# Attention scores of the later blocks as two 64-row products instead of one padded product; first projections 512 columns wide

## The chip, the cores and the metric

The kernel runs on one core of a Trainium2 chip. The metric is the device time of one execution in microseconds (us), the median of several runs. Every time below comes from these runs or from one profiled execution of the kernel before.

## The reference

The model takes 512 tokens of width 1024 through three layers. The first has four mixers (two kinds of attention, two recurrences), a gated merge of them and a mixture of 32 experts. The other two are "hybrid layers", and the change lies in them:

```python
h = rms_norm(x, norm_mix_g)
proj = h @ w_in
rq, rk, rv, rg, pv, nq, nk, nv, mq = jnp.split(proj, 9, axis=-1)       # 256 columns each
# retention on rq, rk, rv, rg; pooling on pv
na = neighbourhood_attention(rms_norm(nq), rms_norm(nk), nv, na_rpb)    # 4 heads of 64
mo = memory_attention(rms_norm(mq), rms_norm(mk), mv)                   # 4 heads of 64, 256 memory rows
up = jnp.einsum('bsnc,ncd->bsnd', branches, w_branch)
gates = jax.nn.sigmoid(h @ w_gate).reshape(b, s, N_BRANCH, dm)
x = x + jnp.einsum('bsnd,bsnd->bsd', gates, up) @ w_out
a, g = jnp.split(rms_norm(x, norm_ffn_g) @ w_ffn_in, 2, axis=-1)
x = x + (jax.nn.silu(a) * g) @ w_ffn_out
```

Both attentions are a softmax of q k / 8 (plus a bias in the neighbourhood) times v. In the neighbourhood attention the 512 tokens are a grid of 8 rows by 64 columns: a block of 8 x 16 queries (128 tokens) sees a window of 8 x 32 keys (256 tokens), so there are 4 blocks.

## The kernel before

Activations lie with features on the partitions, 128 at a time, and tokens along the free axis. A head has 64 features, so one 128-partition tile holds two heads (z = 0 in partitions 0 to 63, z = 1 in 64 to 127).

**Projections.** Weights come by DMA in pieces of 1 MB (`load_w`) and are split into a high and a low part (`split`, L278 on ScalarE, L280 on VectorE). Each product is then three: `mm3` issues L286, L287 and L288. The first projection of a hybrid layer starts while the norm of the layer before it is still running, token tile by token tile: `first_tok(c)` (L1761) takes 512 columns of `w_in` (the keys and values of the retention), as two loads of all 1024 rows by 256 columns, and for each of 4 token tiles adds up two halves of 256 columns in one PSUM bank named `tm`. It is called once per hybrid layer. The bank is 512 columns wide.

**Attention scores.** Two scores, for z = 0 and z = 1, are one product: the query tile is the stationary operand with its 128 partitions (both heads), and the keys stand in a padded tile, `nkz` or `mkz`, that holds keys of z = 0 in partitions 0 to 63 with zeros below, and beside it keys of z = 1 in partitions 64 to 127 with zeros above. The product is 128 rows by 512 columns in one PSUM bank: 256 columns for each head. `nkz` is zeroed by GpSimd (L2142) and filled by ScalarE (L2150, through `proj_tok` and `head_norm`); `mkz` is zeroed (L2236) and filled (L2238) by GpSimd. The neighbourhood score is L2175 (product `ns`), the memory score L2243 (`ms`, its maximum on VectorE at L2246). There are 8 of each in a layer: 4 token blocks times 2 pairs of heads. An fp32 product appears in the trace as two records.

After its score each pair of heads goes through `probs` (L2194): scale, four transposes (`pT`, L2207), and the value products (`po`, L2219), in steps that other work may come between.

**Scores of the first layer.** There the scores of two heads are two products of 64 contracted rows each (L1134, product `s`), into two banks.

**Order.** The merge's products, `gate` (h times w_gate) and `up` (branches times w_branch), are produced by a generator that runs through the whole attention part of a layer; they are 128x512 and three per product. Which instruction stands where on an engine is settled when the program is built: a scheduler orders the instructions by an estimate of their times, by the dependencies and by the order of the code, and the memory attention is issued with raised priority (L1886). Each engine then runs its own list in order and waits at an instruction for what it needs. PSUM has 8 banks, in three groups of buffers: "mm" 2, "ms" 4, "mg" 2 (L2262). Scores, `tm` of the first two token tiles and projections take "mm"; transposes and value products take "ms"; gate and up products take "mg".

Of the kernel before, what the change touches and what calls it, by code (L numbers as in the profile page):

```python
# [210 lines left out]
def backward(a):  # L211

    ap = [list(x) for x in a.ap]
    step, n = ap[-1]
    return bass.AP(tensor=a.tensor, offset=a.offset + step * (n - 1), ap=ap[:-1] + [[-step, n]])


class Kern:
# [1542 lines left out]
    def first_tok(self, c):  # L1761

        Ws = []
        for z in range(2):
            raw = self.load_w([(self.win[:, c + z * 256:c + z * 256 + 256], 0, 256)], KD, 256, z)
            Ws.append([self.split(raw[:, k:k + 4], z) for k in (0, 4)])
        out = []

        def f(i):
            p = self.ps("tm", tag=("mm", "mg")[i // 2])  # L1770
            s = slice(i * 128, (i + 1) * 128)
            for z, W in enumerate(Ws):
                for k in range(KD):
                    self.mm3(p[:, z * 256:(z + 1) * 256], (self.xH[:, k, s], self.xL[:, k, s]), (W[k // 4][0][:, k % 4], W[k // 4][1][:, k % 4]), k == 0, k == KD - 1)
            out.append(p)
        self.first(f)
        return out
# [342 lines left out]
    def neighbourhood(self, l, ctx):  # L2120
        tc, nc = self.tc, self.nc
        pp = ctx.enter_context(tc.tile_pool(name="np2", bufs=1, reuse_waits="tile"))
        f2 = ctx.enter_context(tc.tile_pool(name="nf2", bufs=3, reuse_waits="tile"))
        rp = self.A["rpb2"]
        namask = self.cst4(pp, "namask")[0]

        def biases(z):

            t = pp.tile([128, 8, 4, 32], F32, name="nab", tag="nab", bufs=2)
            for r in range(8):  # L2130
                nc.sync.dma_start(t[r * 16:(r + 1) * 16].rearrange("p a h b -> p (a h) b"),
                                  bass.AP(tensor=rp.tensor, offset=rp.offset + ((l * 15 + 7 - r) * 4) * 96 + 17 + 8 * z, ap=[[1, 16], [96, 32], [1, 32]]))
            for h in range(4):
                nc.vector.scalar_tensor_tensor(t[:, :, h], in0=t[:, :, h], scalar=-1.0,
                                               in1=namask[:, z * 256:(z + 1) * 256].rearrange("p (a b) -> p a b", a=8), op0=OP.mult, op1=OP.add)
            return t
        KS = (0, 8, 24, 32)

        qT = pp.tile([128, 2, 4, 8, 16], F32, name="nqT")

        kz = pp.tile([128, 2, 2, S], F32, name="nkz")
        nc.gpsimd.memset(kz, 0.0)  # L2142
        vT = pp.tile([128, 2, S], F32, name="nvT")
        gq, gk = self.row(pp, f"na_q_norm_g{l}"), self.row(pp, f"na_k_norm_g{l}")
        nc.vector.tensor_single_scalar(gq, gq, -0.125, OP.mult)
        self.proj_tok((1280, lambda i, p: self.head_norm(f2, p, gq, lambda t: [
            nc.scalar.activation(qT[:, j, :, 2 * i:2 * i + 2], t[:, j * 128:(j + 1) * 128].rearrange("p (r b c) -> p b r c", r=2, b=4), AF.Copy)
            for j in range(2)], None)))
        self.proj_tok((1536, lambda i, p: self.head_norm(f2, p, gk, lambda t: [
            nc.scalar.activation(kz[64 * z:64 * z + 64, :, z, i * 128:(i + 1) * 128], t[64 * z:64 * z + 64, 0:256].rearrange("p (a b) -> p a b", a=2), AF.Copy)  # L2150
            for z in range(2)], None)))
        for j, f in enumerate(self.fm(1792, "nv")):
            nc.scalar.activation(vT[:, j], f(), AF.Copy)
        self.flush()
        g8 = lambda t: t.rearrange("p (r c) -> p r c", r=8)
        bias, zb = None, None
        for cb in range(4):
            z = (0, 1, 1, 2)[cb]
            if z != zb:
                bias, zb = biases(z), z  # L2160

            vq = f2.tile([128, 2, 8, 32], F32, name="vq", bufs=2)
            for j in range(2):
                nc.gpsimd.tensor_copy(vq[:, j], g8(vT[:, j])[:, :, KS[cb]:KS[cb] + 32])
            vw = f2.tile([128, 2, 256], F32, name="vw", bufs=2)
            p = self.ps("vw")
            for hf in range(2):
                for j in range(2):
                    o = (hf * 2 + j) * 128
                    nc.tensor.transpose(p[:, o:o + 128], vq[:, j, 4 * hf:4 * hf + 4].rearrange("p r c -> p (r c)"), self.ident)  # L2170
            nc.scalar.activation(vw.rearrange("p a n -> p (a n)"), p, AF.Copy)
            def score(cb, j, bias):
                def f():
                    p = self.ps("ns", tag="mm")
                    nc.tensor.matmul(p, lhsT=qT[:, j, cb].rearrange("p r c -> p (r c)"), rhs=kz[:, j].rearrange("p z (r c) -> p z r c", r=8)[:, :, :, KS[cb]:KS[cb] + 32],  # L2175
                                     start=True, stop=True)
                    t = f2.tile([128, 2, 256], F32, name="nt", bufs=2)
                    mn, rs = (f2.tile([128, 2], F32, name=n) for n in ("nmn", "nrs"))
                    for z in range(2):
                        nc.vector.tensor_tensor_reduce(out=g8(t[:, z]), in0=g8(p[:, z * 256:(z + 1) * 256]), in1=backward(bias[:, :, 2 * j + z]), scale=1.0, scalar=3e38,  # L2180
                                                       op0=OP.add, op1=OP.min, accum_out=mn[:, z:z + 1])
                        nc.scalar.activation(t[:, z], t[:, z], AF.Exp, bias=mn[:, z:z + 1], scale=-1.0, accum_out=rs[:, z:z + 1])
                    return t, rs
                return f

            def done(p, cb=cb):
                H, L = (t.rearrange("p j (r c) -> p j r c", r=8)[:, :, :, cb * 16:cb * 16 + 16] for t in self.ys[2])
                self.done[2] = self.split_act(H, L, p.rearrange("p (j r c) -> p j r c", j=2, r=8))
            sh = []
            for j in range(2):  # L2190
                self.spawn(self.probs(j, f2, sh, score(cb, j, bias), lambda h, k, vw=vw: vw[:, k, h * 64:(h + 1) * 64], done))
        self.flush()
# [31 lines left out]
    def mem_attention(self, l, ctx):  # L2224
        tc, nc = self.tc, self.nc
        kT, v = self.kv[l]
        pp = ctx.enter_context(tc.tile_pool(name="mp2", bufs=1, reuse_waits="tile"))
        f2 = ctx.enter_context(tc.tile_pool(name="mf2", bufs=3, reuse_waits="tile"))
        qT = pp.tile([128, 2, S], F32, name="mqT")
        gq = self.row(pp, f"mem_q_norm_g{l}")  # L2230
        nc.vector.tensor_single_scalar(gq, gq, 0.125, OP.mult)
        self.proj_tok((2048, lambda i, p: self.head_norm(f2, p, gq, qT, slice(i * 128, (i + 1) * 128))))
        self.flush()

        kz = pp.tile([128, 2, 2, 256], F32, name="mkz")
        nc.gpsimd.memset(kz, 0.0)  # L2236
        for z in range(2):
            nc.gpsimd.tensor_copy(kz[64 * z:64 * z + 64, :, z], kT[64 * z:64 * z + 64])  # L2238

        def score(i, j):  # L2240
            def f():
                p = self.ps("ms", tag="mm")
                nc.tensor.matmul(p, lhsT=qT[:, j, i * 128:(i + 1) * 128], rhs=kz[:, j].rearrange("p z n -> p (z n)"), start=True, stop=True)  # L2243
                p = p.rearrange("p (z n) -> p z n", z=2)
                mn, rs = (f2.tile([128, 2], F32, name=n) for n in ("mmn", "mrs"))
                nc.vector.tensor_reduce(mn, p, axis=AX.X, op=OP.max, negate=True)  # L2246
                t = f2.tile([128, 2, 256], F32, name="mt")
                for z in range(2):
                    nc.scalar.activation(t[:, z], p[:, z], AF.Exp, bias=mn[:, z:z + 1], accum_out=rs[:, z:z + 1])
                return t, rs  # L2250
            return f
        for i in range(NT):
            sh = []
            cols = (slice(None), slice(i * 128, (i + 1) * 128))
            for j in range(2):
                self.spawn(self.probs(j, f2, sh, score(i, j), lambda h, k: v[:, k, h * 64:(h + 1) * 64],
                                      lambda p, cols=cols: self.put(3, cols, p.rearrange("p (a b) -> p a b", a=2))))
        self.flush()
# [24 lines left out]
```

## Time and profile before

| | |
|---|---|
| median of 3 runs | 2551.24 us (2550.71 to 2551.85) |
| profiled execution | 2550.32 us |
| span from its first to its last instruction | 2548.6 us |
| TensorE (PE) busy | 2479.9 us, 97% |
| VectorE (DVE) busy | 1086.0 us, 43% |
| ScalarE (ACT) busy | 794.8 us, 31% |
| GpSimd (POOL) busy | 347.9 us, 14% |
| granted TensorE clock, mean | 0.990 of 2.4 GHz |

A time in the trace counts from the first instruction. The recorded duration of a matmul includes its latency, and neighbours overlap: what a product takes of TensorE is read from the distance between the starts of the records around it. "x2" in a row stands for two records run together. The attention of the first hybrid layer lies around 1080 to 1180 us, that of the second around 1890 to 1990 us.

### The profile page before, as it was taken

The numbers are of one execution on the slowest core, as the hardware profiler recorded it, in microseconds if no ns is written. First come the engines' busy times: TensorE is split into PE (matmuls) and PEld (weight loads), VectorE is DVE, ScalarE is ACT, GpSimd is POOL, SyncE is SP. The second block draws the span as 40 slices with busy tenths as digits, with TensorE's granted clock in tenths as the row PEclk, the third lists the DMA queues.
The fourth block names the chain that finished last, engine by engine and source line by source line (L and its number), as shares of the span: only waits on it lengthen the run. The fifth ranks groups of instructions, "written<-read, shape, count | busy, mean of one in ns | idle before, by whom it ended". The sixth has DMA issues, their size and how long they took to land.

```text
span 2548.6 us, 32848 instructions
## 1 busy us (share of the span) xinstructions
PE 2479.9 (97%) x13340; PEld 1954.9 (77%) x13340; DVE 1086.0 (43%) x2002; ACT 794.8 (31%) x1362; POOL 347.9 (14%) x386
## 2 busy tenths in 40 slices
PE   9999999997988989999999999999999999999999
PEld 7788777686545569877788888889877777888887
DVE  3455569645212264344354333226444435433322
ACT  5331234432202233343233322214244223322311
POOL 1201210301102125311200000003421110000000
PEclk9999999998999999999999999999999999999999
DMA  5400321357999932523232322332241332322232
GB/s 159 148 18 18 108 76 50 133 188 279 401 416 353 375 108 79 107 43 107 83 116 83 99 84 93 105 108 75 88 88 51 108 100 99 100 83 93 89 99 83
DMA packets 220124, 324.41 MB, mean 127 GB/s; under 512 B 43384, under 2 KB 176408, under 8 KB 208192
## 3 DMA queue, kind: packets, MB, share of 16 engines
q1 hardware_dynamic: 214784, 311.76, 36.2%
q0 software_dynamic: 5184, 10.50, 1.1%
q8 instruction: 107, 1.75, 0.3%
q14 instruction: 49, 0.40, 0.0%
HBM read 313.81 MB, written 16.80 MB: 130 GB/s over the span
## 4 chain that ended last, share of the span: by engine, by line
PE 61%; DVE 1%; issue 1%; SPq 0%; POOL 0%; ACT 0%; DMA 0%; DVEq 0%; POOLq 0%
PE gate L288 5%; PE gate L286 4%; PE gate L287 4%; PE acc L287 4%; PE acc L286 4%; PE acc L288 4%; PE ffg L287 3%; PE ffg L286 3%; PE ffa L287 3%; PE ffa L286 3%; PE ffg L288 3%; PE ffa L288 3%; PE tm L286 2%; PE tm L288 2%; PE tm L287 2%; PE up L286 1%
## 5 line engine op out<-in xcount | busy, mean ns | idle before, releaser
L280 DVE TENSOR_TENSOR wl<-wraw,wh 128x1024 fp32r<-128x1024 f32 (+1 forms) x336 | 424.6, 1269 | 569.4 <-ACT wh L278 562.2
L278 ACT ACTIVATE wh<-wraw 128x1024 fp32r<-128x1024 f32 (+1 forms) x336 | 354.2, 1059 | 898.3 <-PE gate L287 188.7
L288 PE MATMUL gate<-hH,wl 128*128 128x512 f32 x512 | 204.9, 403 | 5.8 <-DVE wl L280 5.8
L286 PE MATMUL gate<-hH,wh 128*128 128x512 f32 x512 | 207.0, 404 | 0.0
L287 PE MATMUL gate<-hL,wh 128*128 128x512 f32 x512 | 206.7, 404 | 0.0
L1589 PE MATMUL hid<-mraw,xgt 128*64 128x256 f32 x1024 | 126.5, 393 | 16.4 <-DMA mraw<-moe_w_gate 9.0
L286 PE MATMUL acc<-wh,fH 128*128 128x512 f32 x352 | 136.8, 390 | 0.0
L287 PE MATMUL acc<-wl,fH 128*128 128x512 f32 x352 | 136.7, 389 | 0.0
L288 PE MATMUL acc<-wh,fL 128*128 128x512 f32 x352 | 136.6, 389 | 0.0
L286 PE MATMUL tm<-wh,hH 128*128 128x256 f32 x448 | 128.9, 288 | 4.7 <-DVE hn L1807 4.1
L288 PE MATMUL tm<-wh,hL 128*128 128x256 f32 x448 | 127.6, 286 | 0.2 <-DVE hL L296 0.2
L287 PE MATMUL tm<-wl,hH 128*128 128x256 f32 x448 | 126.8, 284 | 0.0
L287 PE MATMUL ffa<-hL,wh 128*128 128x512 f32 x320 | 126.6, 396 | 0.0
L288 PE MATMUL ffa<-hH,wl 128*128 128x512 f32 x320 | 126.6, 396 | 0.0
L286 PE MATMUL ffg<-hH,wh 128*128 128x512 f32 x320 | 126.6, 396 | 0.0
L287 PE MATMUL ffg<-hL,wh 128*128 128x512 f32 x320 | 126.6, 396 | 0.0
L288 PE MATMUL ffg<-hH,wl 128*128 128x512 f32 x320 | 126.6, 396 | 0.0
L286 PE MATMUL ffa<-hH,wh 128*128 128x512 f32 x320 | 126.5, 395 | 0.0
L1589 PEld LDWEIGHTS hid<-mraw,xgt 128*64 128x64 f32 x1024 | 76.1, 141 | 60.9 <-DMA mraw<-moe_w_gate 11.9
L288 PEld LDWEIGHTS gate<-hH,wl 128*128 128x128 f32 x512 | 96.2, 188 | 32.0 <-DVE wl L280 7.5
L286 PEld LDWEIGHTS gate<-hH,wh 128*128 128x128 f32 x512 | 96.2, 188 | 25.7 <-issue 4.2
L287 PEld LDWEIGHTS gate<-hL,wh 128*128 128x128 f32 x512 | 96.2, 188 | 24.7 <-issue 3.8
(600 smaller groups left out, 5109.7 us busy)
## 6 DMA issues: line engine op xcount, KB each, us to landing
wraw<-w_in SPq DMA_DIRECT2D x45, 1024.0 KB, 5.1
wraw<-w_ffn_in SPq DMA_DIRECT2D x44, 1024.0 KB, 5.0
wraw<-w_gate SPq DMA_DIRECT2D x32, 1024.0 KB, 8.1
mraw<-moe_w_gate SPq DMA_DIRECT2D x31, 1024.0 KB, 12.1
mraw<-moe_w_down SPq DMA_DIRECT2D x31, 1024.0 KB, 10.4
mraw<-moe_w_up SPq DMA_DIRECT2D x30, 1024.0 KB, 12.7
wraw<-w_ffn_out SPq DMA_DIRECT2D x20, 1024.0 KB, 5.0
wraw<-w_branch SPq DMA_DIRECT2D x12, 1024.0 KB, 5.5
```

Of the source, the lines that this page charges most:

```text
L278: self.last_split = nc.scalar.activation(H, raw, AF.Copy)
L280: self.after(nc.vector.tensor_sub(L, raw, H.bitcast(F32)), *hold)
L286: m = t.matmul(out, lhsT=lhs[0], rhs=rhs[0], start=first, stop=False)
L287: t.matmul(out, lhsT=lhs[0], rhs=rhs[1], start=False, stop=False)
L288: t.matmul(out, lhsT=lhs[1], rhs=rhs[0], start=False, stop=last)
L1589: m = nc.tensor.matmul(p[r, c], lhsT=lhs[:, k, r], rhs=w(k), start=k == 0, stop=k == KT - 1, skip_group_check=True)
```

## The change

- `first_tok` loads two pieces of 512 rows by 512 columns, splits each in two, and multiplies into the whole 512 columns of the bank at once.
- The neighbourhood's keys stay as they come, in `nkT` (128 partitions, two heads one above the other); a score is two products of 64 rows by 256 columns, each into a bank of its own.
- The memory scores likewise read the keys `kT` directly, and VectorE takes the maximum of each half by itself.

```diff
@@ first_tok
-            raw = self.load_w([(self.win[:, c + z * 256:c + z * 256 + 256], 0, 256)], KD, 256, z)
-            Ws.append([self.split(raw[:, k:k + 4], z) for k in (0, 4)])
+            raw = self.load_w([(self.win[z * 512:z * 512 + 512, c:c + 512], 0, 512)], 4, 512, z)
+            Ws += [self.split(raw[:, k:k + 2], z) for k in (0, 2)]
...
-            for z, W in enumerate(Ws):
-                for k in range(KD):
-                    self.mm3(p[:, z * 256:(z + 1) * 256], (self.xH[:, k, s], self.xL[:, k, s]), (W[k // 4][0][:, k % 4], W[k // 4][1][:, k % 4]), k == 0, k == KD - 1)
+            for k in range(KD):
+                W = Ws[k // 2]
+                self.mm3(p, (self.xH[:, k, s], self.xL[:, k, s]), (W[0][:, k % 2], W[1][:, k % 2]), k == 0, k == KD - 1)
@@ neighbourhood
-        kz = pp.tile([128, 2, 2, S], F32, name="nkz")
-        nc.gpsimd.memset(kz, 0.0)
+        kT = pp.tile([128, 2, S], F32, name="nkT")
...
-        self.proj_tok((1536, lambda i, p: self.head_norm(f2, p, gk, lambda t: [
-            nc.scalar.activation(kz[64 * z:64 * z + 64, :, z, i * 128:(i + 1) * 128], t[64 * z:64 * z + 64, 0:256].rearrange("p (a b) -> p a b", a=2), AF.Copy)
-            for z in range(2)], None)))
+        self.proj_tok((1536, lambda i, p: self.head_norm(f2, p, gk, kT, slice(i * 128, (i + 1) * 128))))
...
-                    p = self.ps("ns", tag="mm")
-                    nc.tensor.matmul(p, lhsT=qT[:, j, cb].rearrange("p r c -> p (r c)"), rhs=kz[:, j].rearrange("p z (r c) -> p z r c", r=8)[:, :, :, KS[cb]:KS[cb] + 32],
-                                     start=True, stop=True)
+                    p = [self.ps("ns", tag="mm") for _ in range(2)]
+                    for z in range(2):
+                        q = slice(64 * z, 64 * z + 64)
+                        nc.tensor.matmul(p[z][:, 0:256], lhsT=qT[q, j, cb].rearrange("p r c -> p (r c)"), rhs=g8(kT[q, j])[:, :, KS[cb]:KS[cb] + 32], start=True, stop=True)
...
-                        nc.vector.tensor_tensor_reduce(out=g8(t[:, z]), in0=g8(p[:, z * 256:(z + 1) * 256]), in1=backward(bias[:, :, 2 * j + z]), scale=1.0, scalar=3e38,
+                        nc.vector.tensor_tensor_reduce(out=g8(t[:, z]), in0=g8(p[z][:, 0:256]), in1=backward(bias[:, :, 2 * j + z]), scale=1.0, scalar=3e38,
@@ mem_attention
-        kz = pp.tile([128, 2, 2, 256], F32, name="mkz")
-        nc.gpsimd.memset(kz, 0.0)
-        for z in range(2):
-            nc.gpsimd.tensor_copy(kz[64 * z:64 * z + 64, :, z], kT[64 * z:64 * z + 64])
...
-                p = self.ps("ms", tag="mm")
-                nc.tensor.matmul(p, lhsT=qT[:, j, i * 128:(i + 1) * 128], rhs=kz[:, j].rearrange("p z n -> p (z n)"), start=True, stop=True)
-                p = p.rearrange("p (z n) -> p z n", z=2)
+                p = [self.ps("ms", tag="mm") for _ in range(2)]
+                for z in range(2):
+                    q = slice(64 * z, 64 * z + 64)
+                    nc.tensor.matmul(p[z][:, 0:256], lhsT=qT[q, j, i * 128:(i + 1) * 128], rhs=kT[q, j], start=True, stop=True)
...
-                nc.vector.tensor_reduce(mn, p, axis=AX.X, op=OP.max, negate=True)
...
-                    nc.scalar.activation(t[:, z], p[:, z], AF.Exp, bias=mn[:, z:z + 1], accum_out=rs[:, z:z + 1])
+                    nc.vector.tensor_reduce(mn[:, z:z + 1], p[z][:, 0:256], axis=AX.X, op=OP.max, negate=True)
+                    nc.scalar.activation(t[:, z], p[z][:, 0:256], AF.Exp, bias=mn[:, z:z + 1], accum_out=rs[:, z:z + 1])
```

Since the scheduler orders the whole program, the change also moves instructions. On TensorE, in the neighbourhood attention of the first hybrid layer, the program before has two neighbouring scores (`ns`) among gates and the transposes of the values (`vw`):

```order
L2175 MATMUL ns_9021<-nkz_8592,nqT_8591 128x512
L286 MATMUL gate_9485<-hH_7452,wh_9481 128x512
L287 MATMUL gate_9485<-hL_7453,wh_9481 128x512
L288 MATMUL gate_9485<-hH_7452,wl_9482 128x512
L286 MATMUL gate_9485<-hH_7452,wh_9481 128x512
L2170 MATMUL vw_9003<-ident_63,vq_8999 128x128 x3
L2175 MATMUL ns_9063<-nkz_8592,nqT_8591 128x512
```

Both heads of a score are in one row. The changed program has, on the same engine and in the same part, half-size scores: `ns_8923` is the second half of one score and `ns_8966` the first half of the next.

```order
L286 MATMUL gate_9400<-hH_7452,wh_9396 128x512
L2174 MATMUL ns_8923<-nkT_8496,nqT_8495 128x256
L287 MATMUL gate_9400<-hL_7453,wh_9396 128x512
L2174 MATMUL ns_8966<-nkT_8496,nqT_8495 128x256
L288 MATMUL gate_9400<-hH_7452,wl_9397 128x512
```

A gate product stands between them. In the memory attention of the same layer, the program before has these rows on TensorE, with two scores (`ms`) around transposes and value products:

```order
L2243 MATMUL ms_10045<-mkz_9947,mqT_9785 128x512
L2219 MATMUL po_10006<-pT_9993,mv0_6754 64x128 x4
L2207 MATMUL pT_10035<-ident_63,mt_10003 128x128 x4
L2219 MATMUL po_10053<-pT_10020,mv0_6754 64x128 x4
L2207 MATMUL pT_10062<-ident_63,mt_10030 128x128 x4
L2243 MATMUL ms_10072<-mkz_9947,mqT_9785 128x512
```

Each score is one row there. In the changed program `ms_9972` is the second half of one score and `ms_10001` the first half of the next; the first half of `ms_9972`'s score stands twelve up products above it, of which four are shown:

```order
L288 MATMUL up_9668<-ysH_7771,wl_9657 128x512
L286 MATMUL up_9668<-ysH_7771,wh_9656 128x512
L287 MATMUL up_9668<-ysL_7772,wh_9656 128x512
L288 MATMUL up_9668<-ysH_7771,wl_9657 128x512
L2238 MATMUL ms_9972<-mkT0_6753,mqT_9700 128x256
L2217 MATMUL po_9982<-pT_9966,mv0_6754 64x128 x4
L2205 MATMUL pT_9991<-ident_63,mt_9954 128x128 x2
L2238 MATMUL ms_10001<-mkT0_6753,mqT_9700 128x256
L2205 MATMUL pT_9991<-ident_63,mt_9954 128x128 x2
L286 MATMUL up_9676<-ysH_7771,wh_9656 128x512
```

The two halves of a score have moved apart, each with 128-row products on at least one side. Over both layers, of the 64 halves 3 stand directly behind another half.

## Rows read from the trace of the kernel before

**Rows 1.** Busy time of each engine in two stretches of time.
```profile
core 0: us, PE busy (x) PEld busy (x) DVE busy (x) ACT busy (x) POOL busy (x), PEclk, DMA share, GB/s
1082.30:1177.30 95.00, 95.00 (x556) 72.34 (x556) 46.48 (x124) 45.35 (x115) 11.84 (x17) 1.00 0.21 56
1892.40:1987.40 95.00, 95.00 (x556) 72.38 (x555) 46.46 (x124) 45.29 (x115) 11.84 (x17) 1.00 0.22 57
```

**Rows 2.** Line groups: busy us, mean ns of one record, idle us before.
```profile
L2175 PE MATMUL ns<-nkz,nqT 128*128 128x512 f32 x32 | 16.4, 593 | 0.0
L2243 PE MATMUL ms<-mkz,mqT 128*128 128x512 f32 x32 | 16.3, 592 | 0.0
```

**Rows 3.** Timeline of TensorE: start, duration, line; a score among gates.
```profile
1109.42 1.02 PE L2175 MATMUL ns<-nkz,nqT 128*128 128x512 f32 x2
1109.88 0.80 PE L287 MATMUL gate<-hL,wh 128*128 128x512 f32 x1
1110.52 0.40 PE L288 MATMUL gate<-hH,wl 128*128 128x512 f32 x1
1110.75 0.39 PE L286 MATMUL gate<-hH,wh 128*128 128x512 f32 x1
```

**Rows 4.** Timeline of TensorE in the first layer: a lone 64-row product.
```profile
400.42 0.39 PE L286 MATMUL gate<-xH,wh 128*128 128x512 f32 x1
400.74 0.70 PE L1134 MATMUL s<-ak,aq 64*128 64x256 f32 x2
401.36 0.50 PE L287 MATMUL gate<-xL,wh 128*128 128x512 f32 x1
401.70 0.39 PE L288 MATMUL gate<-xH,wl 128*128 128x512 f32 x1
401.93 0.40 PE L286 MATMUL gate<-xH,wh 128*128 128x512 f32 x1
```

**Rows 5.** Timeline of TensorE in the first layer: two adjacent 64-row products.
```profile
446.37 0.70 PE L1134 MATMUL s<-ckT,bq 64*128 64x256 f32 x4
447.00 0.50 PE L286 MATMUL gate<-xH,wh 128*128 128x512 f32 x1
```

**Rows 6.** Timeline of TensorE in the first layer: gate, then value products.
```profile
406.20 0.40 PE L287 MATMUL gate<-xL,wh 128*128 128x512 f32 x1
406.53 0.43 PE L1160 MATMUL po<-tt,av 128*64 128x128 f32 x2
```

**Rows 7.** Timeline of TensorE: first and last of three runs of projection products.
```profile
927.59 0.28 PE L286 MATMUL tm<-wh,hH 128*128 128x256 f32 x1
...
928.73 0.28 PE L287 MATMUL tm<-wl,hH 128*128 128x256 f32 x1
...
938.12 0.28 PE L287 MATMUL tm<-wl,hH 128*128 128x256 f32 x1
...
938.83 0.28 PE L287 MATMUL tm<-wl,hH 128*128 128x256 f32 x1
...
1650.05 0.39 PE L287 MATMUL acc<-wl,fH 128*128 128x512 f32 x1
...
1651.86 0.39 PE L286 MATMUL acc<-wh,fH 128*128 128x512 f32 x1
```

**Rows 8.** Line groups on the other engines, from 1015 to 1180 us.
```profile
L2142 POOL MEMSET nkz<- 128x2048 f32 x1 | 1.8, 1808 | 0.0
L2236 POOL MEMSET mkz<- 128x1024 f32 x1 | 1.0, 957 | 18.8 <-PE ns L2175 18.8
L2150 ACT ACTIVATE nkz<-tokT 64x256 f32<-64x256 f32 x8 | 3.0, 377 | 4.0 <-PE tokT L1815 4.0
L2246 DVE TENSOR_REDUCE mmn<-ms 128x2 f32<-128x512 f32 x8 | 5.5, 690 | 9.1 <-PE ms L2243 9.1
```

**Rows 9.** Line group of the first layer's scores, from 382 to 482 us.
```profile
L1134 PE MATMUL s<-ak,aq 64*128 64x128 f32 (+3 forms) x32 | 8.3, 482 | 0.0
```

**Rows 10.** Timeline of VectorE: start, duration, in brackets the wait before.
```profile
1097.39 1.43 DVE L2134 SCALAR_TENSOR_TENSOR nab<-nab,c4namask 128x256 f32<-128x256 f32 x4 [3.59 <-DMA nab<-rpb]
```

## The prediction

> **What bounds the kernel now.** The first view to read is the table of windows over the two stretches in which the edited scores run, 95 us in each of the two later layers. TensorE is busy for 95.00 of 95.00 us in both, at a granted clock of 1.00 (the 2.4 GHz level), while VectorE is busy for 46.5, ScalarE for 45.3 and GpSimd for 11.8 us [rows 1]. So in these stretches only TensorE's time counts, and work taken from or put on the others costs nothing until it makes TensorE wait. The reason is the filler: between the few attention products the merge's gate and up products (128x512, three per product) run without a gap. The second view is the line groups of the two score lines: 32 records each, no idle before either [rows 2]. A score product is two records, so each line stands for 16 products, 32 in all. The third view is the timeline of TensorE, which tells what one product takes of the engine: not its recorded duration, which holds latency, but the distance from start to start of its neighbours.
>
> **The price of one score before.** At 1109.42 a padded score starts, two gate products follow, and at 1110.75 the third one starts: 1.33 us, in which two gate products have 0.23 each (the distance from 1110.52 to 1110.75), so the score took 1.33 - 0.46 = 0.87 us [rows 3]. 32 of them are 27.8 us.
>
> **The price of one half after.** The trace of before has no half of a later score, but block 1 has its exact like: the scores of line 1134, products of 64 contracted rows by 256 columns, two to a score, each into its own bank of tag "mm". At 400.42 a gate starts, at 400.74 a lone 64-row product of two records, and gates at 401.36, 401.70 and 401.93 [rows 4]. From 400.42 to 401.93 are 1.51 us; three gates at 0.23 are 0.69 of it; the lone half took 0.82 us, nearly what the padded whole took. The rows show where it goes: 0.32 instead of 0.23 from the gate to the half, 0.62 in the half, 0.34 instead of 0.23 in the gate behind the next one. So about 0.1 us is lost at either side where the row shape changes, and the same shows between a gate and the value products (0.33 from 406.20 to 406.53) [rows 6].
> The Trainium skill, "TensorEngine Tiling (Array Packing)", Tiling Modes, Key Properties, says that a change of tiling mode drains TensorE; the trace agrees (0.32 to 0.34 against 0.23 at each change), and the rule speaks against a change that enters and leaves such a mode more often.
>
> **What it costs depends on where the halves stand.** If both halves stand next to each other, the second is free: at 446.37 four records (two halves) start, and the gate behind them at 447.00, 0.63 us for both against 0.62 for one [rows 5, 4]. The program's order of the changed kernel decides that, and in every stretch I read the matmuls start in the order in which they stand. The scheduler put other products between the halves: in the places shown with the change, a gate product stands between the last half of one neighbourhood score and the first half of the next, and in the memory part value products and transposes stand between halves of neighbouring scores, and up products between the two halves of one. Counted over both layers, of the 64 halves only 3 stand directly behind another half, so there are 61 separate runs of 64-row work where there were 32 padded products. 61 x 0.82 = 50.0 us against 32 x 0.87 = 27.8 us: **+22.2 us**. Bounds of this term: if a lone half cost only its own 0.62 (its neighbours hiding both changes of shape) it is 61 x 0.62 - 27.8 = +10.0; if it cost as much as a padded product and no two shared, 64 x 0.87 - 27.8 = +27.9. I take 0.82, since that row has the same form and the same neighbours.
>
> **The first projections.** Each of the two calls has 192 products of 128x256, which become 96 of 128x512: 384 become 192. Ten 256-wide products start in 1.14 us (927.59 to 928.73), 0.114 each, and six in 0.71 (938.12 to 938.83), 0.118 each; 512-wide ones elsewhere start eight in 1.81 us (1650.05 to 1651.86), 0.226 each [rows 7]. So one wide product saves 0.002 to 0.010 us over two narrow ones, 192 x 0.002 = 0.4 to 192 x 0.010 = 1.9 us. I take **-0.4**, the longer row. The loads keep their bytes (two of 1 MB per call) and the splits their count and size (four of 128x1024), but the first product now needs a split of two k-tiles by 512 columns where it had four by 256, and the last product needs the second load for k 4 to 7 rather than for the second 256 columns. Both kinds run through the splits in the same order and at the same rate, so no new wait is expected: 0.
>
> **What goes at no gain.** GpSimd's memset in the neighbourhood part (1.8 us) and the one in the memory part (1.0), which itself stood 18.8 us behind a score, are removed with the two copies behind it, and ScalarE's eight copies of keys (3.0 us) become about half as many [rows 8]. TensorE ran through all of these without a gap, so their cover is the gate products, and taking them out is worth 0. VectorE's one maximum over 128x512 (690 ns) becomes two over 128x256: each costs between half and the whole of it, so each of the 16 memory scores takes 0 to 0.69 us more of VectorE, at most 11 us beside the 93 that it is busy in these 190, covered by TensorE again: 0.
>
> **New waits.** A score now takes both banks of "mm" at once where it took one, so the next score's first half waits until VectorE (and for memory ScalarE's exponential) has read the bank; the gates behind it on TensorE wait with it. Not shown in before for these lines. Below: 0.0 us idle before line 1134, which also takes two "mm" banks per score [rows 9]. Above: one maximum at 0.69 us [rows 8] in each of 32 scores, 22.1 us. I take 0, the row of the same form. The bias table's DMA, for which VectorE stands blocked 3.59 us until 1097.39 [rows 10], makes no TensorE wait now, and in the changed order the next product that needs VectorE's work behind it comes some ten gates and more later; 0, with at most those 3.59 us per layer if the filler in front of it runs out.
>
> **The sum.** The profiled execution took 2550.32 us (span 2548.6, 1.7 outside it), 0.9 under the median of 2551.24. 2550.3 + 22.2 - 0.4 = 2572.1, and 0.9 for the median: **2573 us**.
>
> **The rivals.**
> - *The halves share the array* (not slower). Were the second half free in every score, as it is for adjacent ones [rows 5], 32 x 0.82 = 26.2 stand against 27.8: -1.6, with the projections -2.0, 2549 us. For faster beyond that, a pair would have to cost its 0.62 alone: 32 x 0.25 = 8.0, 2543 us. It decides once (64 - n) x 0.82 is below 27.8 + 0.4, n = 30 of the 32 pairs adjacent; 3 are. Against it: the order. For it: only that the halves' records on the chip might meet in spite of what stands between them, which no row shows. Chance 5%: 3% within 0.2% and 2% faster.
>   The Trainium skill, "TensorE: Matmul & The Clock Gate", Part 3, says that products in different row groups run beside each other for a few ns more per tile; the adjacent pair (0.63 against 0.62) agrees, but it helps only neighbours.
> - *Another engine ends the stretch*, so that the longer scores are hidden: 2551 - 0.4, about 2551 us. Against it: 95.00 of 95.00 us. For it: TensorE's waits elsewhere might shrink. Chance 3%.
> - *The two banks stall TensorE*: half of the upper bound, 0.35 us in each of 32 scores, is 11 us more, 2584 us; the whole 22.1, 2595 us. For it: the halves stand among up products that share VectorE with them; against it: 0.0 idle at line 1134. Chance 8%.
> - *The lone half is cheap next to value products and transposes* (fewer changes of shape there, since value products already change it): the lower bound, 2561 us. Chance 12%.
>
> **How the numbers follow.** Forecast 72%, its own range 2566 to 2580; cheap halves 12%, stall 8%, shared array 5%, covered 3%. The range of 8 in 10 reaches from cheap halves (2561, a little inside) to half a stall (2584): 2562 to 2584. What a measurement of this kernel can tell from no change is about 0.2%, 5 us: faster 2%, same 6%, slower 92%.
>
> **What would show it.** In the profile after: the windows of the two score stretches longer by some 11 us each with TensorE still full; 32 records of each score line become 64 in form 64x256, and around a lone one the gates stand 1.5 us apart as in rows 4; the projections' stretch nearly unchanged in length; no idle before the score lines. Idle before the score lines with VectorE or ScalarE as releaser means the stall rival; score stretches within 2 us of their length mean the shared array. The forecast is wrong if a lone half takes clearly less than 0.7 us, or if the time lies within 5 us of before.

## The result: slower by 16 us

The changed kernel took 2566.89 us (median of 4 runs, 2565.44 to 2569.80) beside 2550.97 us for the kernel before (4 runs, 2546.99 to 2551.85). The ratio is 1.0066 with a 95% interval of 1.0054 to 1.0078: slower, by three times the 0.2% that a measurement here can tell. The forecast was 2573, with a range of 2562 to 2584. The direction and the mechanism came out as forecast; the size was 16 us instead of 22. Ratios, here and below, stand with their 95% intervals as measured; they differ a little from the ratios of the medians.

The profiled executions differ by 15.1 us (2565.44 against 2550.32), spans 2563.7 and 2548.6. In the profiled executions of kernels that leave the first layer as it is, that layer and its experts end between 922.3 and 927.7 us, which is several us of chance. So the kernels are compared below by two stretches alone, one for each later layer: from the first transpose of the normed state (`hT`) to the first FFN product. The kernel before, in windows (the stretch, then its length and each engine's busy time):

```profile
core 0: us, PE busy (x) PEld busy (x) DVE busy (x) ACT busy (x) POOL busy (x), PEclk, DMA share, GB/s
924.08:1391.12 467.04, 458.92 (x2613) 384.31 (x2612) 220.54 (x399) 170.87 (x313) 100.11 (x113) 1.00 0.29 83
1729.61:2200.62 471.01, 463.81 (x2636) 387.96 (x2635) 220.89 (x397) 174.91 (x317) 101.56 (x112) 1.00 0.29 87
```

The same stretches of the changed kernel:

```profile
923.83:1397.15 473.32, 466.87 (x2549) 379.87 (x2548) 218.77 (x407) 171.94 (x309) 97.35 (x109) 1.00 0.29 82
1735.63:2215.73 480.10, 474.21 (x2572) 385.49 (x2571) 222.69 (x405) 174.87 (x313) 99.19 (x108) 1.00 0.29 85
```

The two stretches grew by 6.3 and 9.1 us, 15.4 together (938.05 to 953.42), which is the whole difference. TensorE's busy time grew by 18.4 us (922.73 to 941.08) at the same granted clock, and its idle time (length less busy) fell by 3.0 us (15.3 to 12.3). VectorE's busy time stayed in sum (441.4 and 441.5), though the first projections alone take 4.2 us off it (437.3 in E3); that its second maximum costs no time is shown by E1.

The score lines after, by line groups (busy us, mean ns, idle before), answer to [rows 2]:

```profile
L2238 PE MATMUL ms<-mkT,mqT 64*128 64x256 f32 x64 | 22.3, 428 | 0.0
L2174 PE MATMUL ns<-nkT,nqT 64*128 64x256 f32 x64 | 20.2, 428 | 0.0
```

64 records each, and no idle time before either, so no product waits for the second bank. What a lone half takes of TensorE is seen in the timeline of the changed kernel, with the weight loads (PEld) shown too; it answers to [rows 3, 4]:

```profile
1092.67 0.39 PE L286 MATMUL gate<-hH,wh 128*128 128x512 f32 x1
1092.67 0.19 PEld L287 LDWEIGHTS gate<-hL,wh 128*128 128x128 f32 x1
1092.90 0.40 PE L287 MATMUL gate<-hL,wh 128*128 128x512 f32 x1
1093.22 0.29 PEld L2174 LDWEIGHTS ns<-nkT,nqT 64*128 64x128 f32 x2 [0.37 <-issue]
1093.23 0.70 PE L2174 MATMUL ns<-nkT,nqT 64*128 64x256 f32 x2
1093.85 0.19 PEld L288 LDWEIGHTS gate<-hH,wl 128*128 128x128 f32 x1 [0.33 <-issue]
1093.85 0.50 PE L288 MATMUL gate<-hH,wl 128*128 128x512 f32 x1
...
1094.19 0.39 PE L286 MATMUL gate<-hH,wh 128*128 128x512 f32 x1
...
1094.42 0.39 PE L287 MATMUL gate<-hL,wh 128*128 128x512 f32 x1
```

From the gate at 1092.90 to the gate at 1094.42 are 1.52 us; three gates at 0.23 leave 0.83 us for the half, where 0.82 was forecast. The weight loads show why. Between gates, the load of the next product starts together with the product before it (1092.67: load of L287 beside the matmul of L286). Before the half and behind it the load stands still for 0.37 and 0.33 us and starts only with its own matmul: here nothing is loaded ahead across the change of shape.

Beside value products (`po`, 64 output columns) a half is cheaper, as this stretch of the changed kernel shows:

```profile
1107.17 0.43 PE L2217 MATMUL po<-pT,vw 128*64 128x128 f32 x2
1107.54 0.70 PE L2174 MATMUL ns<-nkT,nqT 64*128 64x256 f32 x2
1108.16 0.44 PE L2217 MATMUL po<-pT,vw 128*64 128x128 f32 x4
1108.53 0.70 PE L2174 MATMUL ns<-nkT,nqT 64*128 64x256 f32 x2
1109.16 0.43 PE L2217 MATMUL po<-pT,vw 128*64 128x128 f32 x2
```

Each half takes 0.62 to 0.63 us from its start to the next value product's. The value products change the shape anyway, so a half beside them should add less; how much less is read place by place in E1.

### The profile page after: what moved, and what is told of

Same layout as the page of the kernel before. It is cut to its first block, busy times and chain, and to the rows that moved or that the text cites. A ratio compares the mean times of both kernels' runs of the same rounds, so it can differ in the third digit from the quotient of the medians.

```text
span 2563.7 us, 32562 instructions
## 1 busy us (share of the span) xinstructions
PE 2498.4 (97%) x13212; PEld 1948.3 (76%) x13212; DVE 1085.8 (42%) x2018; ACT 795.3 (31%) x1354; POOL 343.6 (13%) x378
## 4 chain that ended last, share of the span: by engine, by line
PE 68%; DMA 4%; DVE 1%; issue 1%; SPq 0%; POOL 0%; ACT 0%; DVEq 0%; POOLq 0%; ACTq 0%
PE gate L288 5%; PE gate L286 5%; PE gate L287 4%; PE acc L287 4%; PE acc L286 4%; PE acc L288 4%; PE hid L1589 3%; PE ffg L288 3%; PE ffa L288 3%; PE ffa L287 3%; PE ffg L287 3%; PE ffg L286 3%; PE ffa L286 3%; PE tm L286 2%; PE tm L288 2%; PE tm L287 2%
## 5 line engine op out<-in xcount | busy, mean ns | idle before, releaser
L286 PE MATMUL gate<-hH,wh 128*128 128x512 f32 x512 | 204.2, 399 | 0.0
L287 PE MATMUL gate<-hL,wh 128*128 128x512 f32 x512 | 204.1, 399 | 0.0
L286 PE MATMUL acc<-wh,fH 128*128 128x512 f32 x352 | 136.8, 390 | 0.0
L287 PE MATMUL acc<-wl,fH 128*128 128x512 f32 x352 | 136.7, 389 | 0.0
L287 PE MATMUL ffa<-hL,wh 128*128 128x512 f32 x320 | 126.6, 396 | 0.0
L286 PE MATMUL ffg<-hH,wh 128*128 128x512 f32 x320 | 126.6, 396 | 0.0
L287 PE MATMUL ffg<-hL,wh 128*128 128x512 f32 x320 | 126.6, 396 | 0.0
L286 PE MATMUL ffa<-hH,wh 128*128 128x512 f32 x320 | 126.5, 395 | 0.0
L286 PE MATMUL tm<-wh,hH 128*128 128x256 f32 (+1 forms) x384 | 117.3, 307 | 5.0 <-DVE hn L1807 4.5
L288 PE MATMUL tm<-wh,hL 128*128 128x256 f32 (+1 forms) x384 | 117.0, 305 | 0.0
L287 PE MATMUL tm<-wl,hH 128*128 128x256 f32 (+1 forms) x384 | 115.2, 301 | 0.0
L286 PEld LDWEIGHTS gate<-hH,wh 128*128 128x128 f32 x512 | 96.2, 188 | 24.2 <-issue 3.7
L287 PEld LDWEIGHTS gate<-hL,wh 128*128 128x128 f32 x512 | 96.2, 188 | 23.6 <-issue 2.5
```

What stands on the lines that cost most here:

```text
L286: m = t.matmul(out, lhsT=lhs[0], rhs=rhs[0], start=first, stop=False)
L287: t.matmul(out, lhsT=lhs[0], rhs=rhs[1], start=False, stop=False)
L288: t.matmul(out, lhsT=lhs[1], rhs=rhs[0], start=False, stop=last)
```

## The experiments

Each edit is against the changed kernel (E1, E2, and on top of these E6 and E8) or the kernel before (E3 to E5, E7); the medians are of the edited kernel and of the kernel before on the same chip.

**E1, padded halves.** Two products of 256 columns into two banks, as in the change, but with the padded keys, so of 128 rows. The 13212 matmul records of TensorE come in the same order in both traces, with the same 61 runs of scores. The edit of the memory score (the neighbourhood's is alike, and the padded tiles come back):

```diff
-    nc.tensor.matmul(p[z][:, 0:256], lhsT=qT[q, j, i * 128:(i + 1) * 128], rhs=kT[q, j], start=True, stop=True)
+    nc.tensor.matmul(p[z][:, 0:256], lhsT=qT[:, j, i * 128:(i + 1) * 128], rhs=kz[:, j, z], start=True, stop=True)
```

> The changed kernel with the zero-padded keys put back: each score is still two products of 256 columns into two banks, but of 128 rows each. Its order on TensorE has the same 61 runs of score products as the changed kernel. If the 64-row form is what costs (records of 0.31 us and a change of shape on either side), a half is two records of 0.21 us among 128-row products, 64 x 0.43 = 27.5 us against 27.8 before: 2551 us, 2547 to 2555, and the two short waits behind each attention part (0.40 and 1.46 us before) return. If two products apart, two banks, or VectorE's two maxima cost it, the time stays near the changed kernel's: 2563 to 2568 us.

Measured: 2548.03 beside 2548.85 us, ratio 0.9996 (0.9986 to 1.0006). Its two stretches:

```profile
922.54:1385.69 463.15, 457.36 (x2549) 382.86 (x2548) 218.46 (x407) 172.74 (x313) 100.72 (x113) 1.00 0.30 84
1724.18:2193.94 469.76, 464.72 (x2573) 388.65 (x2571) 223.09 (x405) 175.97 (x317) 102.92 (x112) 1.00 0.31 87
```

They are 932.91 us long, 20.5 less than the changed kernel's in the same order, and 19.0 of that is TensorE's busy time (941.08 less 922.08). The timeline of a half in E1, among gates:

```profile
1089.28 0.40 PE L286 MATMUL gate<-hH,wh 128*128 128x512 f32 x1
1089.28 0.19 PEld L287 LDWEIGHTS gate<-hL,wh 128*128 128x128 f32 x1
1089.52 0.39 PE L287 MATMUL gate<-hL,wh 128*128 128x512 f32 x1
1089.52 0.42 PEld L2176 LDWEIGHTS ns<-nkz,nqT 128*128 128x128 f32 x2
1089.75 0.59 PE L2176 MATMUL ns<-nkz,nqT 128*128 128x256 f32 x2
...
1089.99 0.59 PE L288 MATMUL gate<-hH,wl 128*128 128x512 f32 x1
...
1090.41 0.40 PE L286 MATMUL gate<-hH,wh 128*128 128x512 f32 x1
```

From 1089.52 to 1090.41 are 0.89 us, less two gates 0.43 us for the half, and its weight load starts a product ahead of it (1089.52 for 1089.75). So two products apart, two banks and two maxima cost nothing; the 64-row form is what costs. Between value products E1 has these rows:

```profile
1102.29 0.43 PE L2219 MATMUL po<-pT,vw 128*64 128x128 f32 x2
1102.65 0.70 PE L2176 MATMUL ns<-nkz,nqT 128*128 128x256 f32 x2
1103.28 0.44 PE L2219 MATMUL po<-pT,vw 128*64 128x128 f32 x4
```

The padded half takes 0.63 us there, as long as the 64-row half in the same place above: it changes the shape beside value products as well.

Since the order is the same, the two traces can be compared at each of the 61 places, from the start of the product before the scores to the start of the second product behind them. The changed kernel is 0.38 us longer on average at the 40 lone halves with no value product beside them, 0.19 us at 14 with value products on one side and 0.00 us at 4 with value products on both; the 3 adjacent pairs are 0.04 us shorter. That is 17.7 us, the cost of the 64-row form. It agrees with the two score parts as a whole, which are 8.8 us longer in each layer. The other 3 us of the 20.5 lie before the first score of each layer, where both kernels run the same products; 1.5 of them are longer waits of TensorE. From one execution each, those 3 us cannot be told from chance.

The expectation was wrong in one thing: the waits behind the attention parts did not return (below).

**E2, pairs adjacent.** The first half of a score also waits, through a dependency, for the last reader of the bank that the second half will take, so the scheduler finds both ready at once (`m` is the first half's product).

```diff
+    if z == 0:
+        self.behind(m, self.last_read)
...
-    nc.scalar.activation(t[:, z], p[z][:, 0:256], AF.Exp, bias=mn[:, z:z + 1], accum_out=rs[:, z:z + 1])
+    self.last_read = nc.scalar.activation(t[:, z], p[z][:, 0:256], AF.Exp, bias=mn[:, z:z + 1], accum_out=rs[:, z:z + 1])
```

> The changed kernel, with the first half of each score (but the first score of each attention part) made to wait until the second half's bank is free as well, so that the scheduler puts both behind each other: 28 of 32 pairs adjacent, 36 runs of 64-row work where the changed kernel has 61. If each run costs 0.82 us, whether it holds one half or two, 36 x 0.82 = 29.5, less some 0.2 for each of 6 places beside value products, is 28.3 against 27.8 us before: 2551 us, 2548 to 2556. If the halves cost their time one by one, adjacent or not, it stays at 2563 to 2568; if the held half makes TensorE wait, 2557 to 2562 with idle time in front of the score lines.

Measured: 2548.23 beside 2548.85 us, ratio 0.9992 (0.9980 to 1.0004). A pair in its timeline:

```profile
1091.90 0.40 PE L293 MATMUL gate<-hH,wl 128*128 128x512 f32 x1
1092.22 0.30 PEld L2179 LDWEIGHTS ns<-nkT,nqT 64*128 64x128 f32 x4 [0.37 <-DVE wl L285]
1092.22 0.70 PE L2179 MATMUL ns<-nkT,nqT 64*128 64x256 f32 x4
1092.85 0.19 PEld L291 LDWEIGHTS gate<-hH,wh 128*128 128x128 f32 x1 [0.33 <-issue]
1092.86 0.50 PE L291 MATMUL gate<-hH,wh 128*128 128x512 f32 x1
```

Four records, two halves, in 0.64 us from their start to the next gate's, where one half took 0.62; from gate to gate a pair takes 0.82 to 0.84 us at the 12 places where it stands among gates, beside 0.87 for the padded product [rows 3]. The halves that made the kernel slower apart make it no slower when they stand together. Its stretches are 462.48 and 473.42 us, 2.1 less in all than before, and that is what the projections alone give (E3). Two things cancel in this: TensorE's busy time is 3.6 us more than in E3 (923.84 and 920.29), and its idle time as much less, as in E1. Against E1's padded halves, from the first score to the first FFN product, the two layers take 0.4 us more (620.6 and 620.3): paired, the 64-row scores neither gain nor lose.

**E3, projections alone.** The diff's `first_tok` in the kernel before.

> The kernel before with the 512-wide first projections alone. Theory: 0.4 us less to 0.4 more, 2550 to 2552 us. Rival: another order of loads and splits makes its start wait in each of two calls, 2553 to 2556 us.

Measured: 2548.72 beside 2548.85 us, ratio 0.9997 (0.9985 to 1.0008), so the timed runs cannot tell it from nothing. The stretches can:

```profile
927.68:1394.17 466.49, 457.93 (x2518) 376.97 (x2517) 216.54 (x399) 171.10 (x313) 101.83 (x113) 1.00 0.30 83
1732.65:2202.10 469.45, 462.36 (x2541) 381.98 (x2540) 220.74 (x397) 174.96 (x317) 102.34 (x112) 1.00 0.31 87
```

They are 2.1 us shorter than before, 2.4 in TensorE's busy time: outside the expected 0.4 either way, on the good side. TensorE's idle time in them is 15.7 us against 15.3, so the rival's new waits are not there. These are single executions.

**E4, neighbourhood halves alone.** The diff's neighbourhood part in the kernel before.

> The kernel before with the two 64-row products in the neighbourhood scores alone: 28 runs of 64-row work, 12 places beside value products, in place of 16 padded products at 0.87. Theory, with 0.2 us saved at each such place: 28 x 0.82 - 12 x 0.2 - 13.9 = +6.7, less up to 3 us of waits behind the attention that a longer TensorE swallows: 2554 to 2558 us. Without that sharing, +9.1: 2560. If it is the memory part alone that costs (its halves stand among up products), 2551.

Measured: 2555.95 beside 2548.85 us, ratio 1.0025 (1.0014 to 1.0035): +6.4 us by the ratio (+7.1 by the medians), as expected. Its stretches, 8.6 us longer than before:

```profile
924.19:1394.49 470.30, 463.64 (x2630) 384.44 (x2628) 221.28 (x399) 169.89 (x309) 99.79 (x112) 1.00 0.30 83
1732.97:2209.31 476.34, 469.97 (x2652) 389.76 (x2651) 222.45 (x397) 173.94 (x313) 102.15 (x111) 0.99 0.30 86
```

**E5, memory halves alone.** The diff's memory part in the kernel before.

> The kernel before with the two 64-row products in the memory scores alone: 30 runs of 64-row work, 10 places beside value products, in place of 16 padded products at 0.87. Theory: 30 x 0.82 - 10 x 0.2 - 13.9 = +8.7, less up to 3.5 us of waits behind the attention that were also gone with the neighbourhood halves alone: 2554 to 2558 us beside a before of 2549. In the two layers' stretches (first transpose of the normed state to first FFN product, 467.0 and 471.0 us before) the sum grows by 5 to 9 us. If the memory part's halves cost nothing, since they share VectorE and the up products, 2549.

Measured: 2558.07 beside 2550.39 us, ratio 1.0034 (1.0022 to 1.0045), +8.7 us by the ratio (+7.7 by the medians), at the upper end of what was expected; in the stretches +5.8, in the expected 5 to 9. They are:

```profile
922.31:1390.31 468.00, 461.00 (x2630) 383.46 (x2628) 220.19 (x407) 171.16 (x313) 97.93 (x110) 1.00 0.29 83
1728.79:2204.60 475.81, 468.28 (x2652) 389.82 (x2651) 221.74 (x405) 175.19 (x317) 99.23 (x109) 1.00 0.30 86
```

Both score parts cost by themselves. In the stretches E4 is +8.6, E5 +5.8 and E3 -2.1, together 12.2 against 15.4 for the whole change. They do not add up because each kernel has its own order: E4 and E5 have 28 and 30 runs of 64-row work, 58 together, where the changed kernel has 61, and three runs at 0.82 are 2.5 of the 3.1 us. The rest is open.

**E6, E7 and E8, the first layer.** Its scores (line 1134) were 64-row products before the change, some of them apart [rows 4]. The dependency of E2, put there, makes 22 runs of 64-row work 17. E7 is the kernel before with that alone; E6 adds it to E1, E8 to E2.

```diff
+    if z == 0:
+        self.behind(m, self.last_s)
...
-    nc.vector.tensor_tensor_reduce(out=t[:, :nk], in0=p[:, :nk], in1=b, scale=1.0, scalar=3e38, op0=OP.add, op1=OP.min, accum_out=mn)
+    self.last_s = nc.vector.tensor_tensor_reduce(out=t[:, :nk], in0=p[:, :nk], in1=b, scale=1.0, scalar=3e38, op0=OP.add, op1=OP.min, accum_out=mn)
```

> The padded halves of the run before (which have the changed kernel's order), and the first layer's own 64-row scores put behind each other in the way of the adjacent pairs: 17 runs of 64-row work there instead of 22. By 0.82 us for each run that is gone (0.63 to 1.2, since some of these halves are up to 512 columns wide) 3 to 6 us less than the padded halves, so 2542 to 2545 us beside 2548. If the held first halves make TensorE wait in a stretch where VectorE is busy for nine tenths, no gain or a loss: 2547 to 2553.

> The kernel before with the first layer's own 64-row scores put behind each other and nothing else (17 runs of 64-row work there instead of 22; the later layers padded as before). If the gain of the run before came from there (248.5 us from its first score to the first expert product before, 243.3 with the pairs), 5 us less: 2545 beside 2550, ratio 0.997 to 0.999. If it came from the padded halves' order in the later layers, ratio 0.999 to 1.001.

> 64-row scores in all three layers, all put behind each other (36 runs in the later layers, 17 in the first), with the wide first projections: the gain of the first layer's pairs (5 us) and the 0 to 2 us of the adjacent pairs in the later layers: 2543 to 2546 beside 2550, about the same as the padded halves with pairs in the first layer alone (2544). If the held halves stall in one of the three, 2547 or more.

Measured: E6 2544.31 beside 2550.39 us, ratio 0.9968 (0.9955 to 0.9981); E7 2545.09 beside 2551.14, 0.9983 (0.9974 to 0.9992); E8 2543.70 beside 2551.14, 0.9974 (0.9964 to 0.9984). All three came out in the ranges expected and are faster than both kernels; their intervals overlap, so which of them is best stays open. The stretch from the first of these scores to the first expert product, before and in E7:

```profile
383.24:631.70 248.46, 233.87 (x1183) 177.79 (x1183) 162.41 (x390) 91.65 (x187) 41.89 (x38) 0.96 0.46 165
```

```profile
382.07:626.08 244.01, 228.70 (x1184) 176.64 (x1183) 160.59 (x390) 90.71 (x187) 40.72 (x38) 0.96 0.47 168
```

4.5 us shorter, and 5.2 us less TensorE time with the same products. The same stretch takes 243.3 us in E6 and in E8. Five runs of 64-row work are gone, three of 256 columns and two of 512; at 0.83 us and, by an estimate from the rows of the last section, 1.06 + 0.2 us they come to 5.0.

## Why the prediction held, and where its size was off

- **What bounds the stretch.** Right. TensorE's busy time took the cost, VectorE's sum did not move, and idle before the score lines is 0.0.
- **The price of a lone half** (0.82 us, from a lone product of the first layer [rows 4]). Right: 0.83 in the changed kernel. The Trainium skill, "TensorEngine Tiling (Array Packing)", Tiling Modes, Key Properties, has the change of mode drain the engine; the 0.37 and 0.33 us in which no weights are loaded, before and behind a half, agree.
- **The term +22.2.** Too large by a quarter: at the same order the 64-row form cost 17.7 us (the changed kernel against E1, place by place). The step that failed is to price all 61 runs as if among gates. In the changed order scores and value products adjoin 22 times, at 18 of the 61 runs, and there the form costs 0.19 us (one side) or nothing (both) instead of 0.38. With 0.2 us off for each of the 22 the sum is 22.2 - 4.4 = 17.8. The rival of the cheap half beside value products had that mechanism, with 12%, but as an alternative for all halves and not as a share of them, and it counted transposes in, which do not help: a half between two transposes still costs 0.34 us more than in E1.
- **The projections, -0.4.** Mis-sized: -2.1 us in length (E3), beyond the -1.9 of the upper bound. The products themselves give 1.2 of it, inside the bounds: from start to start the 384 narrow ones took 47.4 us before and the 192 wide ones 46.2 in E3. The other 0.9 is not located.
- **New waits, 0.** Right for the scores. But waits elsewhere went, which was not in the sum. Before, TensorE stood still twice right behind the attention of each later layer, 1.9 us in the first and 1.7 in the second; the waits in the first (1080 to 1240 us) of the kernel before:

```profile
PE gate L288 <- DVE wl L280: 1.5, 1, 1.5
PE up L286 <- DVE gth L1242: 0.4, 1, 0.4
```

  The changed kernel has none of them in either layer. I took the longer TensorE work for the reason and expected them back in E1, whose scores are no longer than before. They did not come back: E1's idle time is 10.8 us against 15.3 before. So the order makes them go, not the length: memory scores now stand among the up products (the last pieces of order shown with the change), which before ran in one block behind the last score. But this mixing alone is not enough: E4, with padded memory scores among the up products, has none of these waits, while E5, with halves there, keeps one in each layer (1.1 and 1.5 us). What in the order removes them stays open.
- **The sum.** E1 splits the 15.4 us: +20.5 from E1 to the changed kernel (17.7 for the 64-row form and the 3 before the scores), and -5.1 for all the rest of the change (E1 against before). In these 5.1 TensorE's idle time is 4.5 us less, mostly the waits that the new order hides; its busy time is only 0.6 less, though the projections alone take 2.4 off (E3). What adds the other 1.8 was not isolated; the neighbourhood's value products, which the scores now break up, are busy for 12.4 us in E1 and 10.0 before. So two misses went the same way, 4.5 us for the halves beside value products and 4.7 for the rest of the change, and 3 us that may be chance went the other way: that the size came within 6 us of the forecast is in part luck.
- **The rivals.** The shared array (5%) fell as argued, by the order: E2 shows that it would have held with the pairs adjacent, where by the same sum E2's 28 adjacent pairs lose 1.3 us, too little for the runs to tell from nothing. Another engine ending the stretch (3%) and the bank stall (8%) fell by the idle times. What I said of the windows, 11 us longer each, came out as 6.3 and 9.1.

## What to carry to other kernels

Two half-height products share the array only where they stand behind each other in the program; apart, among 128-row products, each pays nearly the price of the padded product that it replaces (0.83 and 0.87 us here). So before you split a product by rows, count in the built program how many pairs are adjacent, and if a scheduler fills between them, hold the first half until both banks are free. A zero-padded product that keeps the shape of its neighbours was no waste here (E1, ratio 0.9996).

## What was not expected of the hardware

A change between 128-row and 64-row products costs about 0.1 us on either side (0.33 and 0.34 us from start to start instead of 0.23), and the trace shows it as a weight load that starts only with its own matmul (0.37 and 0.33 us without a load) where it otherwise starts one product ahead. More is lost inside the half. The first layer of the kernel before has lone 64-row products of 128 and of 512 columns:

```profile
391.32 0.48 PE L1134 MATMUL s<-ak,aq 64*128 64x128 f32 x2
391.74 0.50 PE L287 MATMUL gate<-xL,wh 128*128 128x512 f32 x1
471.04 1.12 PE L1134 MATMUL s<-ckT,bq 64*128 64x512 f32 x2
472.10 0.50 PE L288 MATMUL up<-ysH,wl 128*128 128x512 f32 x1
```

From its start to the next product's a lone one takes 0.42 us with 128 columns, 0.62 with 256 and 1.06 with 512: 0.21 for each 128 columns and 0.2 that does not grow with them. So of the 0.83 us of a lone half of 256 columns 0.42 goes by its columns, which is what the padded half takes in all among its like (0.43), and some 0.4 by its standing alone in its shape. Beside value products the padded half loses its advantage: between two of them it takes 0.63 us too.
